# Attention: four of the five additions of each pair's running sum become accumulating transfers issued by GpSimd

## The chip, the cores and the metric

The kernel runs on one core of a Trainium2 chip. The metric is the device time of one execution in microseconds (us). The core has five engines that are used here: TensorE (PE in the profile), VectorE (DVE), ScalarE (ACT), GpSimd (POOL) and SyncE (SP), which issues transfers. Each engine runs its own instructions strictly in order, and engines wait for each other, and for transfers, by semaphores. Transfers are carried by 16 DMA engines.

## The reference, cut to what matters

The program is a two-layer backbone (a grouped-query attention layer and a Mamba-2 layer, each followed by a gated feed-forward part). The change touches only the attention of the first layer:

```
def gqa_attend(q, k, v):
    s = jnp.einsum('bqhgd,bkhd->bhgqk', q, k).astype(jnp.float32) * (HEAD_DIM ** -0.5)
    p = jax.nn.softmax(s, axis=-1).astype(v.dtype)
    return jnp.einsum('bhgqk,bkhd->bqhgd', p, v)
```

There are 16 query heads of 64 elements, 4 key/value heads, 512 latent tokens and 256 context tokens. A latent query looks at all 768 keys; a context query looks at the 256 context keys. The softmax needs, for each query, the sum of the exponentials over its keys. Everything is in 32-bit floats.

## The kernel before, in words

The function `attention` handles the heads in eight pairs (class `Pair`, pairs 0 to 7 below). Scores are kept with the keys on the 128 partitions and the queries along the free dimension, so a sum over keys is a sum over partitions and over key tiles. The method `steps` makes seven steps for a pair. Steps t = 0 to 5 take one tile of 128 keys each against 512 latent queries of both heads (a 128x1024 tile); step t = 6 does the context queries. In each step:

- TensorE makes the scores `ps` (lines 835 and 837) in PSUM;
- ScalarE takes their exponential into `pr` (line 838), one of three buffers in turn;
- VectorE adds the tile to a running sum over key tiles: at t = 1 it writes `acc` = tile 0 + tile 1 (line 843), at t = 2 to 5 it adds the new tile to `acc` in place (line 845). There is one buffer for `acc`. At t = 6 a sum of its own, `accc`, is made (line 849);
- one step later TensorE multiplies `pr` by the values (`values`, line 799), and after t = 5 the function `final` multiplies `acc` by a matrix of ones, which adds over the partitions (`ps_sum`, line 805). ScalarE and VectorE then make the reciprocal and scale the output (lines 808 to 812).

Between these steps stands other work, dealt out by a planner (`Weave`, with `Job` and `Light` objects that have costs and due times): the projection of later queries (`ps_q`), their normalisation (`normed`, lines 667 to 692, which moves rows between partitions with four small transfers to `qsw`, line 672), the maxima of the next pair (`maxima`: products `ps_m`, line 761, and reductions on VectorE, line 765), parts of the modulation vectors (`ps_ada`, line 129), and the output projection (`ps_d`, lines 105 to 108, with its addition to X on VectorE, line 1022). Weights for these come in by transfers that SyncE issues. In this part of the kernel a scheduler of the framework sets the order in which instructions stand on each engine, from the order of the calls and its own estimates. GpSimd has no instruction between its last part of the input projection and its first one of the feed-forward part.

Of the kernel before, what the change touches and what calls it, by code (L numbers as in the profile page):

```python
# [11 lines left out]
ALU = mybir.AluOpType  # L12
# [55 lines left out]
def t3(g, name, dt=F32, n=T):  # L68
    return g.t3p.tile([P, n], dt, tag="t3", bufs=g.n3, name=name)
# [442 lines left out]
def attention(g, adas, project, X):  # L512


    nc, I = g.nc, g.I
# [52 lines left out]
    acc = t3(g, "acc", n=L)  # L568
# [175 lines left out]
    class Pair:  # L744
# [45 lines left out]
        def steps(self):  # L790

            (qh, ql), (kh, kl) = qprep[self.p], k2[self.kv]
            po = acc = None
            o = g.t3p.tile([P, T], F32, tag="o", bufs=2, name=f"o{self.p}")

            def values(po, pr, t, off, n, first, last):
                v = vt[t][:, self.kv * HD : (self.kv + 1) * HD]
                for e in range(2):
                    nc.tensor.matmul(po[S64[e], :n], v, pr[:, 512 * e + off : 512 * e + off + n], start=first, stop=last)  # L799

            def final(po, ps, acc, out):

                n = out.shape[-1]
                for e in range(2):
                    nc.tensor.matmul(ps[S64[e], :n], g.ones[:, :HD], acc[:, n * e : n * e + n], start=True, stop=True)
                y, u = t2("y")[:, :n], t2("u")[:, :n]

                nc.scalar.activation(y, ps, AF.Ln)
                nc.scalar.activation(y, y, AF.Exp, scale=-1.0)
                nc.vector.tensor_tensor(out, po, y, ALU.mult)  # L810
                nc.vector.scalar_tensor_tensor(u, ps, -1.0, y, ALU.mult, ALU.mult)
                nc.vector.scalar_tensor_tensor(out, u, 2.0, out, ALU.add, ALU.mult)

            def later_lat(po, pr, t, acc):
                values(po, pr, t, 0, L, t == 0, t == 5)
                if t == 5:
                    final(po, Bk("ps_sum"), acc, o[:, :L])

            def later_ctx(pr, acc):
                pc = Bk("ps_oc")  # L820
                for t in range(2):
                    values(pc, pr, 4 + t, C * t, C, t == 0, t == 1)
                final(pc[:, :C], pc[:, C:], acc, o[:, L:])
                if self.p < 6:
                    nc.sync.dma_start(odram[self.p], o)

            prev = None
            for t in range(7):
                ps, pr = Sb("ps_s"), g.t3p.tile([P, 1024], F32, tag="pr", bufs=3, name="pr")
                for q0, n, k0, off in (((0, L, t * P, 0),) if t < 6 else ((L, C, L, 0), (L, C, L + P, C))):  # L830
                    q, k = slice(q0, q0 + n), slice(k0, k0 + P)
                    outs = [ps[:, 512 * e + off : 512 * e + off + n] for e in range(2)]
                    for i, (a, b) in enumerate(((kh, qh), (kl, qh), (kh, ql))):
                        for e in range(2):
                            nc.tensor.matmul(outs[e], a[S64[e], k], b[S64[e], q], start=i == 0, stop=False)  # L835
                    for e in range(2):
                        nc.tensor.matmul(outs[e], onesr[S64[e]], self.diag[S64[e], q], start=False, stop=True)
                nc.scalar.activation(pr, ps, AF.Exp)
                if t == 0:
                    po = Bk("ps_o")  # L840
                elif t == 1:
                    acc = g.t3p.tile([P, 1024], F32, tag="acc", bufs=1, name="acc")
                    nc.vector.tensor_tensor(acc, prev, pr, ALU.add)
                elif t < 6:
                    nc.vector.tensor_tensor(acc, acc, pr, ALU.add)
                else:
                    acc = t2("accc")
                    halves = pr.rearrange("p (e k q) -> p e k q", e=2, k=2)
                    nc.vector.tensor_tensor(acc.rearrange("p (e q) -> p e q", e=2), halves[:, :, 0], halves[:, :, 1], ALU.add)
                prev = pr  # L850
                yield (lambda t=t, pr=pr, po=po, acc=acc: later_lat(po, pr, t, acc)) if t < 6 else (
                    lambda pr=pr, acc=acc: later_ctx(pr, acc))
            g.o.append(o)
# [866 lines left out]
```

## Time and profile before

| what | value |
|---|---|
| median of 3 runs (lowest, highest) | 1888.05 us (1886.78, 1888.72) |
| span of the profiled execution, first instruction to last | 1884.5 us |
| median less span: what lies around the instructions | 3.55 us |
| TensorE, VectorE, ScalarE, GpSimd busy in the span | 1860.0, 1348.8, 832.6, 232.5 us |
| stretch of the eight pairs | about 112 to 376 us of the span |

The profile is taken from one execution, with times from the start of its span. A row of a group of instructions gives the line of the kernel, the engine, the operation, what it writes and reads, how often it occurs, its busy time in us and the mean in ns of one, and after the second bar the idle time of the engine just before it, with what ended the idle time. Matmuls are pipelined and their ends are modelled, so that TensorE looks busy nearly all the time; where it waits is seen better in the chain of work that ended last, which is followed back from the last instruction, at each step to what released it. PEld is the loading of weights into TensorE. For a transfer the view of DMA issues gives the time from issue to landing.

### The profile page before, as it was taken

Reading aid. Unit: us, or ns where it says so; the run is one execution under the profiler, and the core shown is the slowest. Engines: PE = TensorE matmul, PEld = TensorE weight load, DVE = VectorE, ACT = ScalarE, POOL = GpSimd, SP = SyncE. Lnnn points to the kernel's source line nnn. Section 1 sums busy time; section 2 is a strip of 40 time slices with the busy share of each in tenths; the row PEclk is TensorE's granted clock in tenths of the full one; section 3 lists DMA queues with packets and bytes.
Section 4 is the critical chain, followed back from the end, with each engine's and each line's share of the span. In section 5 each row is a group of like instructions: output and inputs, shape, how many; then the busy total and the mean of one; then the engine's idle time right before and its main releaser. Section 6 shows DMA issues by size and latency. Waiting matters only on the chain.

```text
span 1884.5 us, 27447 instructions
## 1 busy us (share of the span) xinstructions
PE 1860.0 (99%) x10794; PEld 1531.3 (81%) x10794; DVE 1348.8 (72%) x2013; ACT 832.6 (44%) x1422; POOL 232.5 (12%) x220
## 2 busy tenths in 40 slices
PE   9999999999999999999999999999999999999999
PEld 7865545689888888888888888888887888888887
DVE  5688999678877777444478977777888676565655
ACT  3655544354222222222257577766667352323331
POOL 2100000030000000000031243443334200000000
PEclk9999999999999999999999999999999999999999
DMA  9223241015444554222224243434344323323332
GB/s 342 70 82 118 84 145 62 18 50 189 136 134 124 176 180 146 68 68 67 67 79 140 70 121 114 133 113 135 120 126 125 100 78 101 101 87 104 90 101 90
DMA packets 73489, 210.02 MB, mean 111 GB/s; under 512 B 8976, under 2 KB 14480, under 8 KB 73232
## 3 DMA queue, kind: packets, MB, share of 16 engines
q1 hardware_dynamic: 73360, 208.26, 35.2%
q8 instruction: 85, 1.39, 0.3%
q14 instruction: 44, 0.36, 0.1%
HBM read 198.79 MB, written 6.82 MB: 109 GB/s over the span
## 4 chain that ended last, share of the span: by engine, by line
PE 80%; DVE 10%; issue 4%; ACT 3%; DMA 2%; POOL 1%; SPq 0%; DVEq 0%; POOLq 0%; ACTq 0%
PE ps_up L105 10%; PE ps_up L106 10%; PE ps_up L108 10%; PE ps_d L105 6%; PE ps_d L108 6%; PE ps_d L106 5%; PE ps_in L105 4%; PE ps_in L108 4%; PE ps_in L106 3%; PE ps_o L799 2%; PE ps_s L835 2%; PE ps_st L1340 1%; DVE wl L87 1%; DVE xf L1212 1%; PE ps_wo L106 1%
## 5 line engine op out<-in xcount | busy, mean ns | idle before, releaser
L87 DVE TENSOR_TENSOR wl<-wst,wh 128x1024 fp32r<-128x1024 f32 x211 | 261.0, 1237 | 246.5 <-PE ps_up L106 125.4
L85 ACT CAST wh<-wst 128x1024 fp32r<-128x1024 f32 x211 | 220.8, 1048 | 413.5 <-DMA wst<-in_wup 316.2
L106 PE MATMUL ps_up<-hlf,wh 128*128 128x512 f32 x992 | 351.6, 354 | 0.0
L108 PE MATMUL ps_up<-hhf,wl 128*128 128x512 f32 x992 | 351.4, 354 | 0.0
L105 PE MATMUL ps_up<-hhf,wh 128*128 128x512 f32 x992 | 351.2, 355 | 0.0
L105 PEld LDWEIGHTS ps_up<-hhf,wh 128*128 128x128 f32 x992 | 187.5, 189 | 26.2
L106 PEld LDWEIGHTS ps_up<-hlf,wh 128*128 128x128 f32 x992 | 187.6, 189 | 26.0
L108 PEld LDWEIGHTS ps_up<-hhf,wl 128*128 128x128 f32 x992 | 187.5, 189 | 26.1
L105 PE MATMUL ps_in<-hhs,wh 128*128 128x512 f32 (+1 forms) x544 | 199.7, 367 | 0.0
L108 PE MATMUL ps_in<-hhs,wl 128*128 128x512 f32 (+1 forms) x544 | 193.5, 356 | 0.0
L106 PE MATMUL ps_in<-hls,wh 128*128 128x512 f32 (+1 forms) x544 | 193.3, 355 | 0.0
L108 PE MATMUL ps_d<-hdh,wl 128*128 128x512 f32 (+1 forms) x496 | 173.4, 350 | 0.0
L105 PE MATMUL ps_d<-hdh,wh 128*128 128x512 f32 (+1 forms) x496 | 173.3, 350 | 0.1
L106 PE MATMUL ps_d<-hdl,wh 128*128 128x512 f32 (+1 forms) x496 | 172.9, 349 | 0.0
L1022 DVE SCALAR_TENSOR_TENSOR X<-ps_d,mod,X 128x256 f32<-128x256 f32 (+1 forms) x176 | 102.7, 614 | 27.1 <-PE ps_d L108 27.0
L105 PEld LDWEIGHTS ps_in<-hhs,wh 128*128 128x128 f32 x544 | 102.8, 189 | 15.5 <-issue 1.9
L108 PEld LDWEIGHTS ps_in<-hhs,wl 128*128 128x128 f32 x544 | 102.7, 189 | 15.0
L106 PEld LDWEIGHTS ps_in<-hls,wh 128*128 128x128 f32 x544 | 102.9, 189 | 13.0
L106 PEld LDWEIGHTS ps_d<-hdl,wh 128*128 128x128 f32 x496 | 93.2, 188 | 14.4 <-DVE hdl L87 0.2
L108 PEld LDWEIGHTS ps_d<-hdh,wl 128*128 128x128 f32 x496 | 93.2, 188 | 13.1
L105 PEld LDWEIGHTS ps_d<-hdh,wh 128*128 128x128 f32 x496 | 93.0, 188 | 13.0 <-ACT hdh L85 0.3
L168 DVE SCALAR_TENSOR_TENSOR junk<-wada,cb 128x1024 f32<-128x1024 f32 x80 | 97.5, 1218 | 1.1 <-ACT cb L159 0.8
(375 smaller groups left out, 3632.9 us busy)
## 6 DMA issues: line engine op xcount, KB each, us to landing
wst<-in_wup SPq DMA_DIRECT2D x88, 512.0 KB, 3.5
wada<-in_adaT SPq DMA_DIRECT2D x56, 512.0 KB, 3.8
wst<-in_win SPq DMA_DIRECT2D x48, 512.0 KB, 3.6
wst<-in_wdown SPq DMA_DIRECT2D x44, 512.0 KB, 3.7
E<-ad SPq DMA_DIRECT2D x64, 256.0 KB, 6.7
wada<-in_adaB SPq DMA_DIRECT2D x24, 512.0 KB, 4.6
ec<-ead SPq DMA_DIRECT2D x64, 128.0 KB, 4.6
wst<-in_wout SPq DMA_DIRECT2D x16, 512.0 KB, 3.7
```

What stands on the lines that cost most here:

```text
L85: keep(nc.scalar.copy(hi, src))
L87: keep(eng.tensor_tensor(lo, src, _r(hi), ALU.subtract))
L105: mm(out, wh, ah, start=first, stop=False)
L106: mm(out, wh, al, start=False, stop=False)
L108: i = mm(out, wl, ah, start=False, stop=last)
L168: g.tc.keep_in_program_order(nc.vector.scalar_tensor_tensor(junk, w, 1.0, cb[:, v * D : (v + 1) * D], ALU.mult, ALU.mult, accum_out=md[:, ...
L799: nc.tensor.matmul(po[S64[e], :n], v, pr[:, 512 * e + off : 512 * e + off + n], start=first, stop=last)
L835: nc.tensor.matmul(outs[e], a[S64[e], k], b[S64[e], q], start=i == 0, stop=False)
L1022: nc.vector.scalar_tensor_tensor(ap, o[:, c0:c1], gate[:, m, v : v + 1], ap, ALU.mult, ALU.add)
L1212: i = nc.vector.scalar_tensor_tensor(cv, raw[:, tap : tap + n], par(f"sw{tap}", j), cv, ALU.mult, ALU.add)
L1340: nc.tensor.matmul(ps[:, d * 256 : (d + 1) * 256], Bt[:, t * P : (t + 1) * P], xw[d][t], start=t == ts[0], stop=t == ts[-1])
```

## The change

At steps t = 2, 3, 4 and 5 of each pair the addition on VectorE is replaced by a transfer from `pr` to `acc`, issued by GpSimd, that adds what it carries to what stands at its destination:

```
@@ -842,7 +842,7 @@
                     acc = g.t3p.tile([P, 1024], F32, tag="acc", bufs=1, name="acc")
                     nc.vector.tensor_tensor(acc, prev, pr, ALU.add)
                 elif t < 6:
-                    nc.vector.tensor_tensor(acc, acc, pr, ALU.add)
+                    nc.gpsimd.dma_start(acc, pr, accum_op=ALU.add)
                 else:
                     acc = t2("accc")
                     halves = pr.rearrange("p (e k q) -> p e k q", e=2, k=2)
```

The first addition (line 843) and the one of the context queries (line 849) stay on VectorE. Each transfer waits on GpSimd for the exponentials of its step (ScalarE) and for whatever wrote `acc` last: VectorE for the first of a pair, the transfer before it for the other three. What read the result of the addition now waits for the transfer: the matmul `ps_sum` of the pair for the last one. The exponential three steps later, which overwrites the same `pr` buffer, waits for the transfer that reads it as well as for the matmul.

On GpSimd, between the last subtraction of the input projection (`hla`) and the first sum of squares of the feed-forward part (`sqf`), there stood nothing:

```order
L329 TENSOR_TENSOR hla_5_129<-ht,hha_5_128 128x256
L329 TENSOR_TENSOR hla_6_131<-ht,hha_6_130 128x256
L329 TENSOR_TENSOR hla_7_133<-ht,hha_7_132 128x256
L389 TENSOR_TENSOR sqf_3694<-sqf_3694,sqf_3706 128x256
L389 TENSOR_TENSOR sqf_3694<-sqf_3694,sqf_3720 128x256
```

and now the same place on GpSimd has the transfers of all eight pairs:

```order
L329 TENSOR_TENSOR hla_5_129<-ht,hha_5_128 128x256
L329 TENSOR_TENSOR hla_6_131<-ht,hha_6_130 128x256
L329 TENSOR_TENSOR hla_7_133<-ht,hha_7_132 128x256
L845 DMA acc<-pr 128x1024 x32
L389 TENSOR_TENSOR sqf_3694<-sqf_3694,sqf_3706 128x256
L389 TENSOR_TENSOR sqf_3694<-sqf_3694,sqf_3720 128x256
```

Thirty-two transfers have come in, eight times four, and nothing else on that engine has moved.

On VectorE, at the first addition of pair 4 and what follows it (`qs`, `qsq` and `qsw` belong to the normalisation of queries, `ma` and `mb` to the maxima, `mod` and `ada_sb` to the modulation), before:

```order
L843 TENSOR_TENSOR acc<-pr 128x1024
L146 TENSOR_TENSOR mod_89<-ps_adt,par 128x8
L690 SCALAR_TENSOR_TENSOR qsq<-ssq,qsq 128x512
L679 TENSOR_TENSOR qs<-qs,cs 128x512
L680 TENSOR_TENSOR qsw<-qsw,cs 128x512
L845 TENSOR_TENSOR acc<-acc,pr 128x1024
L681 TENSOR_TENSOR qs<-qs,qsw 128x512
L765 TENSOR_REDUCE ma<-ps_m 128x2
L131 COPY ada_sb<-ps_ada 128x512
L690 SCALAR_TENSOR_TENSOR qsq<-ssq,qsq 128x256
L845 TENSOR_TENSOR acc<-acc,pr 128x1024
L765 TENSOR_REDUCE mb<-ps_m 128x2x2
```

and the same place on VectorE now:

```order
L843 TENSOR_TENSOR acc<-pr 128x1024
L146 TENSOR_TENSOR mod_89<-ps_adt,par 128x8
L690 SCALAR_TENSOR_TENSOR qsq<-ssq,qsq 128x512
L679 TENSOR_TENSOR qs<-qs,cs 128x512
L680 TENSOR_TENSOR qsw<-qsw,cs 128x512
L765 TENSOR_REDUCE ma<-ps_m 128x2
L681 TENSOR_TENSOR qs<-qs,qsw 128x512
L131 COPY ada_sb<-ps_ada 128x512
L690 SCALAR_TENSOR_TENSOR qsq<-ssq,qsq 128x256
L691 TENSOR_TENSOR qs<-qs,qy 128x768
L765 TENSOR_REDUCE mb<-ps_m 128x2x2
```

The four additions of the pair are gone from VectorE; the reductions and the parts of the normalisation have moved up, by a place or two in their own order.

On TensorE the matmul `ps_sum` of the end of pair 0 stands where it stood, behind the values of t = 5; the `ps_ada` products behind it have changed places with one matmul of the next scores:

```order
 L799 MATMUL ps_o<-pr,v_755 64x512 x2
 L805 MATMUL ps_sum<-acc,ones 64x512 x2
-L835 MATMUL ps_s<-qh,kh_922 128x512
 L129 MATMUL ps_ada<-wada,sc_83 32x512 x8
-L835 MATMUL ps_s<-qh,kh_922 128x512
+L835 MATMUL ps_s<-qh,kh_922 128x512 x2
 L835 MATMUL ps_s<-qh,kl_923 128x512 x2
```

Whatever stands behind `ps_sum` on TensorE, the next pair's scores first, comes after the last transfer of the pair has landed.

More of the change, by code (lines that the diff above doesn't have):

```diff
@@ L844, in steps @@
                 elif t < 6:
-                    nc.vector.tensor_tensor(acc, acc, pr, ALU.add)
+                    nc.gpsimd.dma_start(acc, pr, accum_op=ALU.add)
                 else:
```

## The prediction

> **What bounds the kernel now.** I read the shares of the engines and of the chain that ended last first, then the stretch in which the change lies, then its groups of instructions, and last the times at which the sums are made and used.
>
> ```profile
> PE 1860.0 (99%) x10794; PEld 1531.3 (81%) x10794; DVE 1348.8 (72%) x2013; ACT 832.6 (44%) x1422; POOL 232.5 (12%) x220
> ...
> PE 80%; DVE 10%; issue 4%; ACT 3%; DMA 2%; POOL 1%; SPq 0%; DVEq 0%; POOLq 0%; ACTq 0%
> ```
>
> TensorE bounds the whole. The eight pairs are another matter. Their stretch, 112 to 376 us, by the busy time of the engines:
>
> ```profile
> core 0: us, PE busy (x) PEld busy (x) DVE busy (x) ACT busy (x) POOL busy (x), PEclk, DMA share, GB/s
> 112.00:376.00 264.00, 258.61 (x1606) 147.94 (x1605) 224.91 (x322) 129.36 (x173) 0.00 (x0) 1.00 0.26 86
> ```
>
> VectorE is busy 225 of 264 us, GpSimd not at all, and TensorE has its full clock. A pair takes 264 / 8 = 33 us. The groups that the change touches, in this stretch:
>
> ```profile
> L838 ACT ACTIVATE pr<-ps_s 128x1024 f32<-128x1024 f32 x56 | 57.1, 1021 | 85.9 <-PE ps_s L837 85.8
> L845 DVE TENSOR_TENSOR acc<-acc,pr 128x1024 f32<-128x1024 f32 x32 | 39.0, 1219 | 6.0 <-ACT pr L838 6.0
> L843 DVE TENSOR_TENSOR acc<-pr 128x1024 f32<-128x1024 f32 x8 | 9.8, 1220 | 1.1 <-ACT pr L838 1.1
> ```
>
> and the chain of work in the stretch, by line, with the share of its 264 us:
>
> ```profile
> by line: PE ps_o L799 13.8%; PE ps_s L835 11.3%; PE ps_d L105 5.8%; PE ps_d L106 4.3%; PE ps_d L108 4.2%; PE ps_m L761 3.9%; PE ps_ada L129 3.3%; issue 3.1%; PE ps_s L837 3.0%; PE ps_q L105 2.7%; DMA wst<-in_wq 2.7%; DVE acc L845 2.6%; DVE
> ```
>
> So the additions that go are 39 us of VectorE, but only 2.6% of 264, 7 us, of the chain. In most of the stretch TensorE's products stand on it, here and there a run of VectorE's work.
>
> **What is removed.** Thirty-two additions, 39.0 us of VectorE. The part that was on the path is worth 7 us. The rest ran beside TensorE and is worth nothing, though instructions queued behind an addition (reductions of the maxima, parts of the normalisation) now come up to 1.2 us earlier; the most that I allow for all this is 10 us. So the gain is 7 us, at most 10, at least 0 if another wait is as late. The first additions, line 843, stay.
>
> **What is added: a chain of four transfers with a due time.** Every transfer waits for the one before it, and the matmul `ps_sum`, at which TensorE stops, waits for the fourth. The room for them is the time from the end of the exponentials of t = 2 (the first addition has nearly always ended by then) to `ps_sum`. The exponentials of t = 2 in pairs 0, 3, 5 and 7, on ScalarE:
>
> ```profile
> 121.05 1.02 ACT L838 ACTIVATE pr<-ps_s 128x1024 f32<-128x1024 f32 x1 [3.31 <-PE ps_s L837]
> 220.57 1.02 ACT L838 ACTIVATE pr<-ps_s 128x1024 f32<-128x1024 f32 x1 [3.37 <-PE ps_s L837]
> 285.96 1.02 ACT L838 ACTIVATE pr<-ps_s 128x1024 f32<-128x1024 f32 x1 [2.12 <-PE ps_s L837]
> 351.86 1.02 ACT L838 ACTIVATE pr<-ps_s 128x1024 f32<-128x1024 f32 x1 [1.11 <-PE ps_s L837]
> ```
>
> and the sums over the partitions of the same pairs, on TensorE:
>
> ```profile
> 140.10 1.03 PE L805 MATMUL ps_sum<-acc,ones 128*64 128x512 f32 x4
> 242.42 1.03 PE L805 MATMUL ps_sum<-acc,ones 128*64 128x512 f32 x4
> 304.36 1.03 PE L805 MATMUL ps_sum<-acc,ones 128*64 128x512 f32 x4
> 370.52 1.03 PE L805 MATMUL ps_sum<-acc,ones 128*64 128x512 f32 x4
> ```
>
> That is 140.10 - 122.07 = 18.0 us, then 20.8, 17.4 and 17.6; all eight pairs (the first, the last, the widest and the tightest stand here) have a mean of 18.8, or **4.7 us for each transfer**. With D the time from one transfer's being free to go to the next one's, TensorE stops for about 4 x D - 18.8 us in each pair once D is over 4.7, and the eight pairs lose 8 x (4 x D - 18.8): 32 us for each us of D. Below that a us or two are lost in pairs 0 and 1, where the fourth transfer by itself has under 4 us: in pair 0 the exponentials of t = 5 end at 136.27 and the sum starts at 140.10, 3.8 us later.
>
> ```profile
> 135.25 1.02 ACT L838 ACTIVATE pr<-ps_s 128x1024 f32<-128x1024 f32 x1 [0.54 <-PE ps_s L837]
> ```
>
> So everything hangs on D, and no row of the trace shows a transfer that accumulates, or one that GpSimd issues. The nearest are the transfers of SyncE in the same stretch (KB each, median us from issue to landing):
>
> ```profile
> q1 hardware_dynamic: 7428, 22.42, 26.1%
> ...
> wada<-in_adaB SPq DMA_DIRECT2D x19, 512.0 KB, 4.7
> ...
> odram<-o SPq DMA_DIRECT2D x6, 384.0 KB, 2.3
> ...
> wst<-in_wq SPq DMA_DIRECT2D x2, 512.0 KB, 3.5
> ...
> qsw<-raw SPq DMA_DIRECT2D x12, 64.0 KB, 2.0
> ```
>
> The first row is a queue's packets, MB and share of the time of 16 engines. 26.1% of 264 us is 68.9 us of all engines for 22.42 MB, so 512 KB (0.524 MB) take 1.6 us in one pass. Without their pass (1.2 and 0.2 us) `odram` has 1.1 and `qsw` 1.8 us of fixed time; `qsw` is the only one from SBUF to SBUF. A plain copy of 512 KB is therefore 1.1 + 1.6 = 2.7 us at the least. An addition in flight has to read the source and the destination, so I count two passes: 1.8 + 3.2 = 5.0 us, or 4.3 with the smaller fixed time. Other transfers share the engines: they are busy 26% of the time, and an overlap costs up to a pass, 0.26 x 1.6 = 0.4 us on average. The row of `wada` against the emptier `wst` (4.7 against 3.5) allows 1.2 us. The ends of D are thus 2.7 and 5.0 + 1.2 = 6.2 us. I take 5.0 + 0.4 = **5.4 us**, by the row from SBUF to SBUF, two passes and the mean overlap.
>
> The loss is 8 x (4 x 5.4 - 18.8) = 22 us.
>
> The Trainium skill, page "DMA: Bandwidth & Descriptors", section on the anatomy of one DMA on the GpSimd path, gives about 2.0 us and the bytes over 436 GB/s, which for a copy of 512 KB is an estimate of 3.2 us; the page "Collectives: The Full Stack", section on the bandwidth ceiling, says that an add in flight halves the rate because it reads two sources, which makes 4.4 us of it. By these two D would stay under 4.7, the loss at nothing and the time at 1888 - 7 = 1881. No row here shows either.
>
> **What else waits.** On GpSimd nothing is queued behind a waiting transfer but the next ones; its next other work is in the feed-forward part, after the last sum. On ScalarE the exponentials of three steps later wait for the transfer that reads their buffer; with steps (369.7 - 114.1) / 55 = 4.65 us apart this bites only when D is near 7 us.
>
> ```profile
> L838 ACT ACTIVATE pr<-ps_s x56: 1004/1024/1026, 114.1 to 369.7; 128x1024 f32<-128x1024 f32 x56
> ```
>
> The weight loads of SyncE meet more traffic: 32 x 3.2 us is 102 of 264 us, so the engines' share goes from 26% to about 65%. On the chain there are six places where a transfer is waited for; its first, its longest and its last are these (start, us):
>
> ```profile
> 135.43 2.00 DMA qsw<-raw
> ...
> 207.94 6.74 DMA qsw<-qs
> ...
> 316.82 3.61 DMA wst<-in_w_o
> ```
>
> Each may lose about a pass, 1.6 us, in two cases of five (102 of 264), and six of them 4 us. Against that, while TensorE stops, VectorE catches up with what it would have been late with; I give this the same 4 us, an estimate. What moved in VectorE's and TensorE's order is a place or two of the same work, and counted at nothing.
>
> **Sum.** Loss 22, gain 7, the two of 4 us cancel: +15 us. The profiled execution has a span of 1884.5 us, the median of the runs lies 3.55 above it, and the same 15 us go on the median: 1888 + 15 = **1903 us**.
>
> **The rivals.** *The transfers fit.* If D is 4.3 (two passes on the fixed time of `odram`) or less, the chain keeps its due time but for a us or two in pairs 0 and 1, and VectorE's 7 us are won: 1888 - 7 + 2 = 1883, at best 1888 - 10 = 1878. For it speaks the row of `odram`, 384 KB in 2.3 us; against it the rows of SBUF to SBUF, and that GpSimd has to make the transfer's list first. The two pages of the Trainium skill above are on its side. *A wash.* With D from 4.8 to 5.05 the loss is 3 to 11 us against 7 of gain: 1884 to 1892, so 1888. *The lock.* If GpSimd can't write a transfer's list while VectorE holds their common way into SBUF, each issue waits up to one long VectorE instruction, 1.22 us by the row of line 845, and VectorE is busy 70% of the time even without the additions ((225 - 39) / 264). D is then up to 5.4 + 1.2 = 6.6, the loss 61 us and the time 1888 + 61 - 7 = 1942. The Trainium skill, page "SBUF — State Buffer", has this trap for fp32 copies, but says that an addition of two tensors does not hold the way for writing. The changes of sign between all these lie at D = 4.9 us.
>
> **How the numbers follow.** A measurement of this kernel can tell about 0.2%, 3.8 us, from no change. Chances: forecast (D from 5.05 to 6.2) 0.38, the transfers fit 0.30, a wash 0.22, the lock 0.10. Of the second a part, 0.02, gains too little to be told. So faster 0.28, same 0.24, slower 0.48. The likeliest case by itself is 1892 (D = 5.05) to 1929 (D = 6.2). The range goes down to 1880, to take in the fits, and up to 1932; the lock and the best of the fits are left out.
>
> **What would show it.** Right: in the profile after, `ps_sum` waits for a transfer in all eight pairs, some 3 us each; the transfers land 5 us or more after their issue; line 845 is gone from VectorE, which is busy about 186 us in the stretch; the stretch is some 15 us longer and everything after it as long as before. Wrong: a landing under 4.7 us with no wait before `ps_sum` and a shorter stretch (the transfers fit), or landings over 6.5 us that grow when VectorE is busy (the lock).

## The result and the profile after

| | median, us (lowest to highest) | runs |
|---|---|---|
| before | 1887.62 (1886.78 to 1888.72) | 4 |
| after | 1946.12 (1942.16 to 1948.10) | 4 |

The ratio is 1.0304, with a 95% interval of 1.0291 to 1.0316: the change costs 58.5 us, where 15 were forecast, and the time lies above the range. The profiled execution has a span of 1946.0 us against 1884.5. Nearly all of the 61.5 us between these two lies in the stretch of the pairs, which has gone from 264 us to 321. It begins at 112 us in both, and from its end to the end of the program there are 1508.5 us before and 1513.0 after. Of these 4.5 us, 2.7 are the pairs' too: their last sum (`ps_oc`, line 805) starts at 374.73 us before, 1.27 ahead of the end of the stretch, and at 434.47 after, 1.47 behind it. By the busy time of the engines:

```profile
core 0: us, PE busy (x) PEld busy (x) DVE busy (x) ACT busy (x) POOL busy (x), PEclk, DMA share, GB/s
112.00:433.00 321.00, 270.93 (x1584) 152.99 (x1585) 188.17 (x286) 129.83 (x171) 27.88 (x32) 0.91 0.50 121
```

VectorE has lost 37 us of work, as intended (188 against 225), GpSimd has 28 us of writing transfers out, the DMA engines' share has gone from 0.26 to 0.50, and TensorE's granted clock, 1.00 before, has a mean of 0.91. TensorE had 5 us without work in this stretch and now has 50. The waits in the stretch (total us, times, longest) say for what:

```profile
POOL acc L845 <- DMA acc<-pr: 76.3, 15, 8.6
...
PEld ps_sum L805 <- DMA acc<-pr: 45.0, 7, 12.4
PE ps_sum L805 <- DMA acc<-pr: 42.2, 7, 11.5
```

Seven of the eight sums wait for the fourth transfer, 42 us in all. The groups of the addition and of the sum, which answer to line 845 on VectorE before:

```profile
L845 POOL DMA_DIRECT2D acc<-pr x32 | 27.9, 871 | 326.4 <-ACT pr L838 186.1 <-DMA acc<-pr 76.3 <-DVE wl L87 23.0
...
L805 PE MATMUL ps_sum<-acc,ones 128*64 128x512 f32 x32 | 14.7, 1018 | 42.2 <-DMA acc<-pr 42.2
```

The second row has a second piece of news: a matmul of the sum takes 1018 ns in the mean, where each took 592 before. The transfers of the stretch (KB each, median us from issue to landing; the queues' shares of the time of 16 engines):

```profile
q0 software_dynamic: 4608, 16.78, 28.2%
q1 hardware_dynamic: 7288, 21.86, 21.1%
...
acc<-pr POOLq DMA_DIRECT2D x32, 512.0 KB, 4.6
wada<-in_adaB SPq DMA_DIRECT2D x19, 512.0 KB, 6.8
...
qsw<-qs SPq DMA_DIRECT2D x16, 64.0 KB, 2.3
```

GpSimd's queue takes 28.2% of 321 us for 32 transfers, 2.83 us of all engines for each. SyncE's loads of 512 KB for `wada` land 6.8 us after their issue, and did so after 4.7 before. A quiet pair is seen best on GpSimd in pair 6, where no load is met:

```profile
372.39 0.86 POOL L845 DMA_DIRECT2D acc<-pr  x1 [23.04 <-DVE wl L87]
377.54 0.86 POOL L845 DMA_DIRECT2D acc<-pr  x1 [4.28 <-DMA acc<-pr]
382.74 0.88 POOL L845 DMA_DIRECT2D acc<-pr  x1 [4.34 <-DMA acc<-pr]
387.94 0.87 POOL L845 DMA_DIRECT2D acc<-pr  x1 [4.32 <-DMA acc<-pr]
```

Issues are 5.15 to 5.2 us apart: 0.86 us in which GpSimd writes the transfer out, some 3.65 until it has landed (4.50 to 4.57 from the start of the issue), 0.64 until the next one starts. Its sum starts 20.5 us after the end of the exponentials of t = 2 and had to wait 2.97 us. Pair 4 is the other kind:

```profile
284.44 1.01 ACT L838 ACTIVATE pr<-ps_s 128x1024 f32<-128x1024 f32 x1
```

Its exponentials of t = 2 end at 285.45 and its sum starts at 314.71, 29.3 us later. All pairs, with the room that the sum left before, what it took after, the mean time from issue to landing of the pair's four transfers, and TensorE's idle time ahead of the sum (us):

| pair | 0 | 1 | 2 | 3 | 4 | 5 | 6 | 7 |
|---|---|---|---|---|---|---|---|---|
| room before | 18.0 | 18.4 | 20.8 | 20.8 | 19.4 | 17.4 | 18.0 | 17.6 |
| time after | 23.3 | 25.7 | 26.9 | 30.8 | 29.3 | 21.5 | 20.5 | 20.9 |
| mean landing after | 5.1 | 5.3 | 5.9 | 7.0 | 6.7 | 4.8 | 4.5 | 4.6 |
| TensorE idle after | 0 | 3.4 | 7.4 | 9.9 | 11.5 | 3.9 | 3.0 | 3.1 |

Pairs 5 to 7 are what the forecast had for all eight: D is 21.0 / 4 = 5.2 and the wait some 3 us. Pairs 1 to 4 are not: 28.2 / 4 = 7.0. Most of that is late landings. In pair 1 some 2.6 us of the 25.7 are not: its third and fourth transfers were issued 2.35 and 1.34 us after the landing before them, instead of some 0.55, because their exponentials came late.

### The profile page after: what moved, and what is told of

It is laid out like the page before. It is cut to its first block, busy times and chain, and to the rows that moved or that the text cites. A ratio compares the mean times of both kernels' runs of the same rounds, so it can differ in the third digit from the quotient of the medians.

```text
span 1946.0 us, 27490 instructions
## 1 busy us (share of the span) xinstructions
PE 1875.5 (96%) x10794; PEld 1538.1 (79%) x10794; DVE 1314.9 (68%) x1981; ACT 833.8 (43%) x1422; POOL 258.7 (13%) x252
## 4 chain that ended last, share of the span: by engine, by line
PE 69%; DVE 4%; ACT 2%; DMA 2%; issue 1%; POOL 0%; SPq 0%; DVEq 0%; POOLq 0%; ACTq 0%
PE ps_up L105 10%; PE ps_up L106 10%; PE ps_up L108 10%; PE ps_d L105 5%; PE ps_d L108 5%; PE ps_d L106 5%; PE ps_in L105 4%; PE ps_in L108 4%; PE ps_in L106 4%; PE ps_st L1340 1%; PE ps_wo L106 1%; PE ps_yo L1405 1%; PE ps_wo L108 1%; PE ps_wo L105 1%; PE ps_first L106 1%
```

## The experiments

**Theory.** The chain of transfers is late at the sum, as forecast, but two things make it dearer: transfers that meet SyncE's loads, and TensorE's clock, which falls around the waits. **Rivals.** *Order*: the moved instructions are a worse order by themselves. *Crowding*: the transfers take engines from the loads and the moved rows, and the waits at the sum only shift that loss. *Lock*: GpSimd and VectorE hold each other up. Each time is a median beside runs of the kernel before on the same chip (1888.0 to 1888.6 us); the ratio is to these.

### No additions at all

```
-                    nc.gpsimd.dma_start(acc, pr, accum_op=ALU.add)
+                    pass
```

> The additions of t = 2 to 5 are left out altogether (no transfer, no VectorE addition; the sum holds tiles 0 and 1 alone, and the logarithm has a small bias so that it stays finite). This prices the relief of VectorE by itself. My theory (a gain of 7 us from the chain, then lost to the waits for the transfers and to TensorE's clock): 1878 to 1883 us, clock full. A rival, that the new order of the work is itself worse and part of the 58 us comes from there: 1888 us or more.

Measured: 1883.59 us, ratio 0.9980 (0.9971 to 0.9990), just above the range of the theory. Its stretch:

```profile
112.00:374.00 262.00, 257.84 (x1615) 149.00 (x1616) 190.05 (x292) 131.60 (x173) 0.00 (x0) 1.00 0.27 88
```

TensorE is as full as before, at full clock. In this stretch its order and VectorE's are those of the changed kernel but for a few places. So the order is no worse, and the relief of VectorE is worth 4.8 us. That is also about the most that a way of getting these additions off VectorE can bring while this order stands.

### The same transfers as plain copies

```
-                    nc.gpsimd.dma_start(acc, pr, accum_op=ALU.add)
+                    nc.gpsimd.dma_start(acc, pr)
```

> The same 32 transfers from GpSimd as plain copies (acc is overwritten, nothing is added; the logarithm has a small bias so that it stays finite). If the second read of the destination is what makes a transfer long (a share of the engines of 2.8 us against 1.6 for a pass), a copy lands 1.2 us sooner, 3.3 us after its issue, the next is issued 4.0 us after the one before, the chain fits its 4.7 us a transfer in the quiet pairs, and the time falls to 1885 to 1900 us. If GpSimd's way of issuing is what costs, a copy lands 4.2 us or more after its issue and the time stays over 1930 us.

Measured: 1900.93 us, ratio 1.0073 (1.0058 to 1.0088), just above the 1885 to 1900 of the first case. The queue and the landing, in the window from 112 to 400 us:

```profile
q0 software_dynamic: 4608, 16.78, 15.3%
...
acc<-pr POOLq DMA_DIRECT2D x32, 512.0 KB, 2.9
```

A copy takes 15.3% of 288 us / 32 = 1.38 us of all engines and lands after 2.9 us; the addition in flight takes 2.83 and lands after 4.6, 4.5 where nothing is met. So it is twice a copy in engine time, which agrees with what the Trainium skill's page "Collectives: The Full Stack", section on the bandwidth ceiling, says of an add in flight. With copies the four steps fit in pairs without loads, and TensorE's waits at the sums, 42 us with accumulating transfers, are 8.3 in all, the longest 4.3 in pair 4. Of the 62.5 us between no transfers and accumulating ones, 17.3 are there with copies already.

### Half the columns on VectorE

```
-                    nc.gpsimd.dma_start(acc, pr, accum_op=ALU.add)
+                    nc.vector.tensor_tensor(acc[:, :512], acc[:, :512], pr[:, :512], ALU.add)
+                    nc.gpsimd.dma_start(acc[:, 512:], pr[:, 512:], accum_op=ALU.add)
```

> VectorE adds columns 0 to 511 of each tile in place as before, GpSimd's accumulating transfers take columns 512 to 1023. A whole transfer has 2.8 us of the engines' time and 1.7 us of fixed time to its landing, and 0.64 us to the next issue. If the bytes set the length, a half lands after 1.7 + 1.4 = 3.1 us and the chain runs at 3.75 us, under the 4.7 that there are: waits only where other transfers are met, time 1890 to 1905. If the fixed part is the larger one, it lands after 4 us or more, the chain runs at 4.6 and over and the time is 1915 or more.

Measured: 1895.41 us, ratio 1.0035 (1.0021 to 1.0048). The accumulating transfer of 256 KB:

```profile
acc<-pr POOLq DMA_DIRECT2D x32, 256.0 KB, 3.3
```

It lands 3.25 to 3.33 us after its issue in 17 of the 32 cases, against 4.5 for 512 KB. So an accumulating transfer here is about 2.0 us fixed and 1.25 for each 256 KB; with 0.64 to the next issue a step of the chain is 3.9 us, below the 4.7 of room, and most of the loss is gone. What is left, 7 us over before, is not a matter of the chain's length in quiet pairs.

### TensorE kept busy in the wait

Ahead of the sum, 16 needless matmuls of 128 columns on `pr`, which it has already:

```
-                    final(po, Bk("ps_sum"), acc, o[:, :L])
+                    ps = Bk("ps_sum")
+                    [nc.tensor.matmul(ps[:, :P], g.ones, pr[:, :P], start=True, stop=True) for _ in range(16)]
+                    final(po, ps, acc, o[:, :L])
```

> The changed kernel with 16 matmuls of 128 columns that nobody needs (about 4 us) ahead of each sum over the partitions, in its own bank and on the exponentials of t = 5, so that TensorE works through the wait. If the half clock that follows each wait costs as much as I think, the spells of half clock go in pairs 0, 1, 5, 6 and 7, whose waits are 3 to 4 us, and the time falls by 8 to 15 us to 1931 to 1938, although work is added. If the half clock costs nothing (TensorE is not what is waited for just then), the time is 1946 or up to 10 us more.

First the sight that led to it. In the kernel after, around the wait of pair 2 (the sum starts at 227.19 us):

```profile
209.00:219.00 10.00, 10.00 (x69) 5.58 (x69) 4.79 (x5) 4.23 (x6) 1.74 (x2) 1.00 0.70 168
...
222.00:232.00 10.00, 4.81 (x14) 1.21 (x14) 2.33 (x4) 1.95 (x4) 0.00 (x0) 0.50 0.51 137
232.00:245.00 13.00, 11.88 (x84) 7.77 (x85) 10.94 (x17) 6.72 (x10) 0.87 (x1) 1.00 0.28 69
```

The granted clock (third number from the end) is 1.00, then 0.50, then 1.00 again. There is one such spell in each of the eight pairs, between 3.4 and 13.7 us long and each a multiple of 3.41; together they are 61.4 us, partly wait and partly work at half speed. In pairs 2 to 7 it begins in the wait ahead of the sum or at its end. In pairs 0 and 1 it belongs to earlier waits, 3.3 and 2.85 us for VectorE; the wait of 3.42 us ahead of the sum of pair 1 has none. The kernel before has no wait of TensorE over 2 us in this stretch and no spell. The busy time in the eight spells added up:

```profile
sum 61.43, PE 38.16 PEld 19.37 DVE 18.39 ACT 11.42 POOL 2.52; mean PE 4.77 PEld 2.42 DVE 2.30 ACT 1.43 POOL 0.31
```

TensorE works for 38 of the 61 us. At full clock the same work would take about half (a matmul of the sum, 592 ns before, has a median of 1061 in the kernel after), so the half clock can have cost some 19 us at most. The Trainium skill's page "TensorE: Matmul & The Clock Gate", part 1, has this as the array's clock being gated to half after an idle window of some 3.4 us; the trace agrees in the half and in 3.41 as the unit, but the window need not be idle here. Laid from spell to spell in steps of 3.41 us, the stretch of the kernel after falls into windows; in the one ahead of each spell TensorE was busy for 1.6 us or less, and in every other window at full clock for 1.67 or more. So what decides here is about half a window of work, and where the borders lie. The other runs have the limit at about the same place, but for one spell of the kernel with GpSimd's additions, behind 2.6 us of work. In pair 1 these are the window ahead of the spell and the two between which the later wait of 3.42 us is cut (TensorE's busy time is the number behind the length of 3.40):

```profile
167.20:170.60 3.40, 1.10 (x10) 1.08 (x12) 2.59 (x5) 0.00 (x0) 0.00 (x0) 1.00 0.82 154
...
180.90:184.30 3.40, 1.72 (x17) 0.70 (x14) 3.27 (x8) 1.02 (x1) 0.00 (x0) 1.00 1.00 177
184.30:187.70 3.40, 1.67 (x12) 0.48 (x16) 0.03 (x1) 0.54 (x1) 0.00 (x0) 1.00 0.62 248
```

Measured: 1939.38 us, ratio 1.0275 (1.0259 to 1.0290), about 7 us less than the kernel after although 128 matmuls were added; 8 to 15 were expected. What still waits is pairs 2 to 4:

```profile
PE ps_sum L805 <- DMA acc<-pr: 16.8, 3, 7.2
```

and the half-clock spells have shrunk to 20.5 us. The clock is thus a real term, of about 7 us or more, but not the main one. A version with a filler for every pair (17, 36, 42 or 50 matmuls by the pair):

> As the run with needless matmuls ahead of the sum, but with their number by pair (17 in pairs 0, 1, 5, 6 and 7, then 36, 42 and 50 in pairs 2, 3 and 4), so that TensorE works through the longest waits too. The spells of half clock that were left go (20 us, from 61 with no such matmuls). If half clock costs about as much in pairs 2 to 4 as it did in the others, the time falls by another 3 to 8 us, to 1931 to 1936; what is then left over the kernel before, some 45 us, is waits and late transfers. If it is the half clock that makes most of the loss, the time falls below 1920.

It had 10.2 us of half clock and 1939.72 us, ratio 1.0270 (1.0256 to 1.0284): no further gain, where 3 to 8 us were expected. In pairs 0, 1 and 4 the filler outlasts the wait by 2 to 4 us, so this run can't say how much of the rest is clock.

### The sum asked for one step later

```
-                if t == 5:
-                    final(po, Bk("ps_sum"), acc, o[:, :L])
...
-            def later_ctx(pr, acc):
+            def later_ctx(pr, acc, po, sums):
+                final(po, Bk("ps_sum"), sums, o[:, :L])
```

> The changed kernel with the sum over the partitions of a pair asked for one step later, with the context queries' values, so that the chain of four transfers has about 4.6 us more room. If the due time of the chain is what costs, the waits before the sum go in pairs 0, 5, 6 and 7 (20.5 to 23.3 us from the exponentials of t = 2 to the sum, against 23.4 of room) and shrink by 4.6 us in pairs 1 to 4; waits fall from 42 to about 12 us and the time to 1895 to 1910. If the transfers cost by what they take from other transfers (weights and moved rows that come late), the time stays over 1930.

Measured: 1925.81 us, ratio 1.0203 (1.0180 to 1.0226), and the waits that remain:

```profile
PE ps_sum L805 <- DMA acc<-pr: 20.1, 4, 7.1
```

It lies in neither of the two ranges: above 1895 to 1910, with 20 us of waits and not 12, and below 1930. Pairs 5 to 7 follow each other at 34.6, 33.8 and 30.0 us, about as before (31.4, 36.1, 30.1), so a step more of room is enough for the quiet chain; the other pairs keep waits of 5.1, 7.0 and 7.1 us and lose the rest. To price the order by itself, the kernel before got the same later sum:

> No accumulating transfer at all: the kernel before with the sum asked for one step later, nothing left out. It prices the later sum by itself, after pairs 2 and 3 of e10_quiet, without any transfer in them, took 38.8 and 38.1 us where the kernel before has 35.0 and 33.5. Theory A (the later order is the cost there): 1893 to 1899 us with the same two long pairs. Theory B (the later order is free, and e10_quiet lost to its transfers): 1886 to 1890 us.

That took 1894.96 us, ratio 1.0033 (1.0021 to 1.0046): the later order costs 6.8 us with no transfer in it, the time of the first theory. The two long pairs that this theory named don't show: in the profiled execution, the fastest of ten at 1889.25 us, pairs 2 and 3 took 36.1 and 35.9 us, and not 38.8 and 38.1, so where the 6.8 us lie isn't seen. So the transfers cost 31 us of the later sum's 1925.8, against 58.5 where it stood.

### What a met load costs

Three needless transfers of 512 KB, issued by SyncE at t = 4 in each of the quiet pairs 5 to 7:

```
+                    [nc.sync.dma_start(g.dp.tile([P, 1024], F32, name=f"dead{self.p}{i}"), pr)
+                     for i in range(3 * (t == 4 and self.p > 4))]
```

> The changed kernel with three needless transfers of 512 KB from the exponentials of t = 4 to DRAM, issued by SyncE, in pairs 5, 6 and 7 alone, where the accumulating transfers were undisturbed. If it is meeting SyncE's transfers that makes them land after 7 to 11.6 us in pairs 0 to 4, the transfer of t = 4 or 5 of pairs 5 to 7 now lands after 8 to 10 us instead of 4.5, the wait before the sum grows by 3 to 5 us in each, and the time by 10 to 20 us, to 1956 to 1966. If the long landings come from something else in pairs 0 to 4 (VectorE's load, say), the landings of pairs 5 to 7 stay near 4.5 and the time near 1946.

Measured: 1952.50 us, ratio 1.0338 (1.0323 to 1.0354), 6.4 us more than the kernel after. The accumulating transfers that meet these land after 5.6 to 6.3 us, and TensorE's waits in the three pairs grow from 10.0 to 14.5 us. The direction is as expected, the size below it. In the pairs with real loads the meetings are worse, because SyncE sends those in bursts. The kernel after, on SyncE ahead of the sum of pair 3:

```profile
258.58 3.40 SPq L123 DMA_DIRECT2D wada<-in_adaB  x6
```

and the DMA engines while the fourth transfer of that pair is under way (issued at 261.07, landed at 272.66 us):

```profile
261.00:272.70 11.70, 1.79 (x18) 0.77 (x14) 3.58 (x9) 1.02 (x1) 0.87 (x1) 0.72 0.94 276
```

Six loads, 3 MB, in 3.4 us; then the engines are 94% busy and the transfer takes 11.6 us. Ahead of the sum of pair 2 it is four loads from 215.39 us on, and 10.0 us.

Not every late landing is a burst, though. TensorE's longest wait, 11.5 us in pair 4, comes after a chain whose third transfer, issued at 300.64 us, landed after 8.84. The queues in just this time:

```profile
q0 software_dynamic: 144, 0.52, 29.9%
q1 hardware_dynamic: 144, 0.52, 25.9%
q8 instruction: 1, 0.02, 0.8%
```

It met one load of 512 KB and one packet of the queue that the view calls instruction, and the engines were busy only 57% of the time. The load has 25.9% of 8.84 us, 2.3 us of all engines; the packet, at 0.8% of 16 engines, 1.1 us of one. Together that is 3.4 of the 4.3 us by which the landing is late. In quieter places the packet alone shows. The transfer issued at 337.12 us (pair 5) landed after 5.53 us, one of the two in pairs 5 to 7 that took over 4.6, with no transfer of SyncE under way:

```profile
q0 software_dynamic: 144, 0.52, 50.5%
q8 instruction: 1, 0.02, 1.4%
```

That 1.4% of 16 engines for 5.53 us is 1.2 us of one engine, and the landing is 1.0 us late. The transfers issued at 249.75 and 412.14 us, 0.7 and 0.4 us late, are like it. This fits a transfer that is spread over the engines and has landed only when the last of them is through, but no run varies these packets.

### Transfers whose result nobody waits for

The sum reads the exponentials of t = 5 and not `acc`; the 32 transfers stay as they are, in their chains:

```
-                    final(po, Bk("ps_sum"), acc, o[:, :L])
+                    final(po, Bk("ps_sum"), pr, o[:, :L])
```

> All 32 accumulating transfers stay as they are, in the same chains, but the sum reads the exponentials of t = 5 instead of acc, so no engine waits for a transfer's result (left out: tiles 0 to 4 of the sum; the logarithm gets a tiny bias). Theory (waits at the sum, the clock after them and what follows from them are most of the loss; what the transfers take from other transfers is 6 to 14 us): 1889 to 1900 us, no spell of half clock over 3.4 us, quiet landings still 4.5 us. Rival (the loss is mostly contention: late loads and late small transfers, with the waits at the sum only shifting it): 1915 us or more, with TensorE waiting for moved rows and loads in pairs 0 to 4.

Measured: 1898.10 us, ratio 1.0054 (1.0033 to 1.0075), so good to some 4 us. The stretch:

```profile
112.00:390.00 278.00, 264.61 (x1638) 152.85 (x1637) 193.79 (x299) 134.32 (x177) 27.92 (x32) 0.99 0.58 145
```

This parts the loss in two. Crowding by itself is 1898.1 - 1883.6 = 14.5 us; the waits at the sum with all that follows from them are 1946.1 - 1898.1 = 48.0; the 4 us are the uncertainty of both. The rival of crowding as the main cause falls, but its size is over three times what the forecast had. Where it comes from is seen in the waits of VectorE from 112 to 176 us. This row is in the kernel before:

```profile
DVE qs L679 <- DMA qsw<-qs: 0.6, 1, 0.6
```

and this one in the kernel with the unread sum; the kernel after has the same 5.2:

```profile
DVE qs L679 <- DMA qsw<-qs: 5.2, 1, 5.2
```

It is a move of 64 KB rows in pair 1. In the kernel before, from 150 to 165 us, its four parts land so:

```profile
DMA to landing us min/median/max: 1.9/2.0/2.0
```

and in the kernel after, from 150 to 185 us:

```profile
DMA to landing us min/median/max: 1.9/2.0/4.5
```

One small part, issued at 161.2 us behind the accumulating transfer of 160.65, makes VectorE wait 4.6 us longer in its normalisation, and TensorE behind it. Against the kernel without additions the unread sums start 3.7 us late in pair 0, 9.1 in pair 1, and 12.1 to 12.8 in pairs 4 to 7, so the quiet pairs lose next to nothing. One spell of half clock, 6.8 us, longer than the 3.4 expected, follows a wait of 2.85 us for VectorE in pair 1.

### The additions on GpSimd itself

```
-                    nc.gpsimd.dma_start(acc, pr, accum_op=ALU.add)
+                    nc.gpsimd.tensor_tensor(acc, acc, pr, ALU.add)
```

> GpSimd makes the additions of t = 2 to 5 itself (tensor_tensor in place), with no transfer. By the row of its additions of 128x768 (1852 ns) one of 128x1024 takes 2.4 us, up to 3.5 where VectorE is in its way, so the chain fits its 4.7 us each. If the transfers and what they meet are the whole loss, this has the relief of VectorE without it: 1882 to 1887 us. If GpSimd's additions slow VectorE's (both read the same memory), VectorE's rows of 1.22 us grow and the time is 1890 or more.

Measured: 1901.43 us, ratio 1.0067 (1.0054 to 1.0080). Nobody waits for GpSimd's additions (2.3 to 3.1 us each) before the sum, but VectorE's own operations with two inputs stretch while they run:

```profile
164.42 2.46 DVE L681 TENSOR_TENSOR qs<-qs,qsw 128x512 f32<-128x512 f32 x1
...
172.16 2.77 DVE L692 SCALAR_TENSOR_TENSOR qs<-qsq,qs 128x768 f32<-128x768 f32 x1
```

In the kernel without additions these two take 0.68 and 0.95 us. GpSimd's additions just then:

```profile
163.97 2.36 POOL L845 TENSOR_TENSOR acc<-acc,pr 128x1024 f32<-128x1024 f32 x1 [2.52 <-ACT pr L838]
171.75 2.36 POOL L845 TENSOR_TENSOR acc<-acc,pr 128x1024 f32<-128x1024 f32 x1 [5.42 <-ACT pr L838]
```

Each of the two operations of VectorE began while one of these ran and ended 0.6 and 0.8 us after it, about its own length. So the lock exists for GpSimd's arithmetic, and the time is the rival's. For its transfers it does not show in the kernel after: GpSimd wrote 31 of the 32 out in 0.85 to 0.89 us each, as if nothing held it up, the first in 1.01, and ten of the twelve in pairs 5 to 7 land after 4.5 to 4.6 us, though VectorE is busy for most of the time, as in pair 6:

```profile
371.00:392.50 21.50, 18.55 (x106) 11.18 (x104) 13.19 (x19) 6.85 (x9) 3.47 (x4) 1.00 0.56 114
```

VectorE (the third engine) has 13.2 of 21.5 us there, and the four landings are 4.50 to 4.57 us.

### Transfers in the quiet pairs alone

First with the later sum in all pairs, then with it in pairs 5 to 7 only (and in both, VectorE's additions in pairs 0 to 4):

```
-                    nc.gpsimd.dma_start(acc, pr, accum_op=ALU.add)
+                    (nc.gpsimd.dma_start(acc, pr, accum_op=ALU.add) if self.p > 4
+                     else nc.vector.tensor_tensor(acc, acc, pr, ALU.add))
```

> Nothing is left out: accumulating transfers only in pairs 5 to 7, where SyncE loads little; VectorE's additions in pairs 0 to 4; the sum asked for one step later in all pairs. Theory (the chain fits where no load is met and the sum is asked for a step later; relieving VectorE is worth at most 4.8 us over eight pairs, so 1 to 2 over three): 1885 to 1890 us, ratio 0.998 to 1.001, pairs 5 to 7 at about 34.6, 33.8 and 30.0 us. Rival (the transfers cost something even there, or the later sum costs something by itself): 1893 us or more.

> Nothing is left out: pairs 0 to 4 are those of the kernel before, the sum included; pairs 5 to 7 have the accumulating transfers and the later sum. Theory (the transfers fit in these pairs and the relief of VectorE is 1 to 2 us over three): 1885.5 to 1889 us, ratio 0.998 to 1.000, pairs 5 to 7 at about 32.6, 33.8 and 30.8 us. Rival (the transfers cost something there too): 1891 us or more.

The first took 1896.80 us, ratio 1.0044 (1.0030 to 1.0057): its rival, and the cost points to the later order in pairs 0 to 4, since the kernel before with that order alone has 1894.96 and the two intervals overlap. The second took 1889.36 us, ratio 1.0008 (0.9999 to 1.0017), just above the 1889 of its theory. Its last sums wait for next to nothing:

```profile
343.44 1.08 PE L805 MATMUL ps_sum<-acc,ones 128*64 128x512 f32 x4
373.43 1.08 PE L805 MATMUL ps_sum<-acc,ones 128*64 128x512 f32 x4 [0.90 <-DMA acc<-pr]
```

So where no load is met and the sum is asked for a step later, the transfers cost nothing that a measurement can tell, and they gain nothing either. None of the kernels that compute the whole beat the one before.

## Why the prediction was wrong

The mechanism was right, and it was the likeliest of the cases: the chain of four transfers passes its due time, `ps_sum` waits, and what lies behind the pairs stays as long as it was but for 2 us. One of its signs did not come: 19 of the 32 landings are under 4.6 us and not 5 or more, because the step from a landing to the next issue makes up the rest of D. The size was not right: 58.5 us for 15. The runs give a ladder from before to after, against the terms of the forecast:

| term | forecast | measured | by |
|---|---|---|---|
| relief of VectorE | -7 | -4.8 | no additions, against before |
| other transfers late, catch-up | +4 - 4 | +14.5 | unread sum, against no additions |
| waits at the sum, and what follows | +22 | +48.0 | after, against unread sum |
| sum | +15 | +57.7 | after, against before: +58.5 |

(The last two differ by 0.8 us because the medians of before beside these runs do, 1887.62 and 1888.38.)

- **Two passes and a fixed time, 5.0 us.** Right: 5.15 in quiet pairs, for partly other reasons. The passes are cheaper (2.5 us for 3.2, by the two sizes), the fixed time is 2.0 for 1.8, and 0.64 us from a landing to the next issue, which the sum didn't have, is the rest. The estimate of 4.4 from two pages of the Trainium skill ("DMA: Bandwidth & Descriptors", anatomy of one DMA, and "Collectives: The Full Stack", the bandwidth ceiling) is borne out by the quiet landing of 4.5; what it lacked is that in a chain the step to the next issue comes on top, and 4.5 + 0.64 is over the 4.7 of room.
- **"0.26 x 1.6 = 0.4 us on average" for an overlap: the step that failed.** It took loads as spread evenly and a meeting as costing a pass at most. The 32 landings have a mean of 5.5 us, a whole us over the quiet 4.5, and single ones reach 11.6, above all because SyncE's loads come in bursts of up to six. So the overlap costs 1.0 us for each transfer and not 0.4: at the forecast's own 32 us for each us of D that is 32 us of loss and not 13. In pairs 1 to 4 the time for a transfer is 7.0 us, over the 6.2 that was taken as the end of D. With the times after of all eight pairs, 24.9 us in the mean, the forecast's own formula gives 8 x (24.9 - 18.8) = 49 us. That this comes so near to the measured 48.0 is partly luck: pair 0 is in it without a wait at its sum, and the 48 have the clock in them.
- **The clock had no price at all.** Eight of TensorE's nine waits of 2.8 us and more have work at half speed around or behind them. That costs about 7 us or more by the filler, and some 19 at most by the work done in the spells.
- **"The two of 4 us cancel" failed too.** The late moved rows and loads cost 14.5 us even where no sum waits, most of it in pairs 0 and 1, and there was no catch-up to set against it.
- **The relief, 7 us by the chain of before, was 4.8.** The row of the chain was a fair guide to it.
- **The rivals.** The fits and the wash were out once D passed 4.9. The lock gave 1942 us, close to what came, but for a reason that isn't there: landings do not grow with VectorE's work. A close number is no proof of its story.

Open stays how the 48.0 us divide between waiting and half clock: the waits at the sums are 42.2 by the profile, the half clock 7 to 19, and the two can't be added up, since some of each runs beside other delays. Open, too, is why copies, which cost half the engine time, still lose 17.3 us over no transfers; waits at the sum (8 us) and late rows are both in it, and no run parts them.

## What to carry to other kernels

A chain of dependent transfers is priced by its room at the place where its result is read, link by link: fixed time, bytes, and the step from a landing to the next issue; and the traffic that it meets is read from the bursts in which loads are issued at that place, not from the mean share of the engines. Before work is taken off an engine that isn't the bound, leave the work out and time that: here it showed 4.8 us as the most that could be had. A wait put ahead of TensorE can cost more than its length: here the clock fell to half around eight of nine waits of 2.8 us and more.

## What the runs showed of the hardware

- An accumulating transfer of 512 KB from SBUF to SBUF, issued by GpSimd, takes 0.86 us of GpSimd, lands 4.5 us after its issue and uses 2.83 us of the 16 engines; of 256 KB it lands after 3.25. A plain copy of 512 KB takes 0.53 us of GpSimd, lands after 2.9 and uses 1.38.
- Among six loads of 512 KB the same accumulating transfer took 11.6 us, and a move of 64 KB behind one 4.5 and 5.75 instead of 2.0.
- Three accumulating transfers of 512 KB that met no other data, but one packet of 0.9 to 1.2 us on the queue that the view calls instruction, landed after 4.9, 5.2 and 5.5 us instead of 4.5.
- TensorE's granted clock in the kernel after was 0.50 in spells of 3.4 to 13.7 us around or just behind waits of 2.85 us and more, in steps of 3.41 us; one wait of 3.42 us had none. In the kernel after each spell followed a window of 3.41 us with at most 1.6 us of work on TensorE; no window at full clock with 1.67 or more was followed by one.
- An addition of 128x1024 on GpSimd took 2.3 to 3.1 us and stretched VectorE's operations with two inputs from 0.68 to 2.46 and from 0.95 to 2.77 us.
